# A 8192 x 8192 float32 transpose: eight column ranges of 16 KB regions and a looped TensorE program become four ranges of 32 KB regions, two load buffers, SyncE transfers and a written-out TensorE program

## The chip, the core and the metric

The kernel runs on one core of one Trainium2 chip. TensorE (PE), VectorE (DVE), ScalarE (ACT), GpSimd (POOL) and SyncE (SP) each run their own instruction stream and meet through semaphores; 16 DMA engines move data between HBM and SBUF, and every transfer here is cut into packets that are spread over all 16. The metric is the device time of one execution in microseconds, less is better.

## What is computed

The reference transposes a matrix and does nothing else:

```python
x = np.random.randn(8192, 8192).astype(np.float32)
def reference(x): return np.transpose(x)
```

256 MB are read and 256 MB are written.

## The kernel before

**Chunks.** The input is cut into 128 chunks of 128 rows by 4096 columns (2 MB each): the left half of the columns from top to bottom (64 chunks), then the right half. `chunks` (line 98) lists them. A load (lines 100 to 104) brings one chunk to SBUF, one row of 16 KB to each of the 128 partitions. There are three load buffers (`NIN`, line 65); the first three loads are issued by SP, all later ones by ACT, each after TensorE has finished the chunk that last used the buffer (lines 241 to 243), so load t+3 waits for chunk t.

**Transposes.** TensorE transposes a chunk in 32 blocks of 128 x 128 against an identity (line 118). Block b of a range takes every fourth column (`B` = 4), so that one partition of the result holds four output rows that lie side by side in HBM. The results of 16 transposes fill one half of PSUM (four banks); there are two halves, e = 0 and e = 1. TensorE's program is a loop, `turns` (lines 138 to 149), whose body holds the transposes of three chunks and is run 43 times; the waits are on semaphores that it counts down itself.

**Copies and regions.** ACT copies half 0 out of PSUM and DVE half 1 (line 228) to `regs`, nine regions of 16 KB per partition (`NREG`, line 66). The 4096 columns of a chunk are eight ranges q of 512 columns, and each range has one region open at a time. A region collects eight chunks (`W`), so that each output row piece is 8 x 128 x 4 B = 4 KB long. The ranges are staggered: range q closes when c mod 8 equals q (line 195), so one region closes, and one 2 MB store is issued, in every chunk. The ninth region is the one being stored; a range that reopens waits for the store that used the region last (lines 201 and 202). A window that runs over the end of the left half is stored in two parts. The first windows and the last ones are shorter.

**Stores.** `store` (line 160) issues on ACT, between its copies. `wide_dma` (line 20) hands the source to the transfer as one contiguous run per partition, and the destination as rows, so a 2 MB store reads 16 KB per partition and writes four rows of 4 KB. The very first store is an ordinary one.

So ACT's order of work in a chunk is: wait for PSUM and for a region, copy half 0, issue a store, wait for TensorE, issue a load. All loads from the fourth on, and all stores, go through ACT's one transfer queue and are taken in order. SBUF per partition: 3 x 16 KB of load buffers and 9 x 16 KB of regions, 192 KB.

Of the kernel before, what the change touches and what calls it, by code (L numbers as in the profile page):

```python
# [24 lines left out]
def wide_dma(nc, eng, queue, out, in_):  # L25


    return eng.add_instruction(
        mybir.InstDMACopy(
            mode="Copy",  # L30
            name=nc.get_next_instruction_name(),
            engine=eng.engine,
            ins=[physical(in_)],
            outs=[physical(out)],
            queue=queue,
        )
    )
# [3 lines left out]
def kernel(  # L41
# [5 lines left out]

    nc = tc.nc
    P = 128
    N, M = x.shape
    assert x.shape == out.shape[::-1]
    dt = x.dtype

    S = 32
    B = 4
    W = 8
    NR = S // B
    NIN = 3
    NREG = 9
    CH = N // P
    J = S * P

    with tc.tile_critical():  # L70
        nc.alloc_sbuf_tensor("pad", [P, 32], dt)
        ident = nc.alloc_sbuf_tensor("ident", [P, P], dt).ap()
        ins = [nc.alloc_sbuf_tensor(f"in{k}", [P, J], dt).ap() for k in range(NIN)]
        SIZE = B * W * P
        regs = nc.alloc_sbuf_tensor("regs", [P, NREG * SIZE], dt).ap()
        NH = NR // 2
        pss = [nc.alloc_psum_tensor(f"ps{k}", [P, NH * B * P], dt).ap() for k in range(2)]

        s_id = nc.alloc_semaphore("s_id")
        s_ld = [nc.alloc_semaphore(f"s_ld{k}") for k in range(NIN)]  # L80
        s_st = [nc.alloc_semaphore(f"s_st{k}") for k in range(NREG)]
        s_bank = [nc.alloc_semaphore("s_banka"), nc.alloc_semaphore("s_bankv")]
        s_pe = nc.alloc_semaphore("s_pe")
        s_cp = [nc.alloc_semaphore("s_cpa"), nc.alloc_semaphore("s_cpv")]

        nc.gpsimd.memset(ident, 0.0).then_inc(s_id, 1)  # L86
        nc.gpsimd.wait_ge(s_id, 1)
# [1 line left out]
            out=ident,  # L89
            in_=ident,  # L90
            compare_op=mybir.AluOpType.not_equal,
            fill=1.0,
            base=0,
# [1 line left out]
            channel_multiplier=1,  # L95
        ).then_inc(s_id, 1)

        chunks = [(s, c) for s in range(M // J) for c in range(CH)]

        def load(t):  # L100
            s, c = chunks[t]
            (nc.sync if t < NIN else nc.scalar).dma_start(
                out=ins[t % NIN], in_=x[c * P:(c + 1) * P, s * J:(s + 1) * J]
            ).then_inc(s_ld[t % NIN], 16)

        def transposes(k):
            nc.tensor.sem_inc(s_ld[k], -16).wait_op(s_ld[k], 16, "sem-ge")
            for q in range(NR):
                e, g = divmod(q, NH)
                if g == 0:
                    nc.tensor.sem_inc(s_bank[e], -1).wait_op(s_bank[e], 1, "sem-ge")  # L116
                for b in range(B):
                    tr = nc.tensor.transpose(  # L118
                        pss[e][:, (g * B + b) * P:(g * B + b + 1) * P],
                        ins[k][:, q * B * P + b:(q + 1) * B * P - B + b + 1:B],  # L120
                        ident,
                    )
                if q % 2:
                    tr.then_inc(s_pe, 1)

        T = len(chunks)
        assert T % NIN == NIN - 1
        pe = [nc.tensor.engine]  # L130
        for e in range(2):
            nc.tensor.sem_inc(s_bank[e], 1)
        nc.tensor.wait_ge(s_id, 2)

        turn = nc.alloc_registers("turn", engines=pe)
        nc.regs_mov(turn, 0)
        nc.br("turns", engines=pe)
        with nc.body("turns", valid_engines=pe):
            now = nc.snap(turn, min_val=0, max_val=T // NIN)
            with nc.tensor.If(now < 3):  # L140
                hint = nc.tensor.mark_branch_hint_location()
            with nc.tensor.If(now > 0):
                transposes(NIN - 1)
            for k in range(NIN - 1):
                transposes(k)
            nc.regs_alu(turn, turn, 1, op=mybir.AluOpType.add)
            nc.tensor.br_lt(
                turn, T // NIN + 1, on_true="turns", on_false="done"
            ).branch_hint(hint)
        nc.switch_bb("done")  # L150

        for t in range(NIN):
            load(t)

        copied = [0, 0]
        free = list(range(NREG))
        stored = [0] * NREG
        window = {}

        def store(q, e, count):  # L160
            t0, r, parts = window.pop(q)
            nc.scalar.wait_ge(s_cp[e], count)
            base = 0
            for s, a, z in parts:
                rows = (z - a) * P
                j0 = s * J + q * B * P
                dst = out[j0:j0 + B * P, a * P:a * P + rows]
                dst = dst.rearrange("(q b) i -> q b i", q=P)
                src = regs[:, r * SIZE + base:r * SIZE + base + B * rows]
                base += B * rows  # L170
                if any(stored):
                    st = wide_dma(nc, nc.scalar, "qActDynamicHW", dst, src)
                else:
                    st = nc.scalar.dma_start(
                        out=dst, in_=src.rearrange("q (b i) -> q b i", b=B)
                    )
                st.then_inc(s_st[r], 16)
                stored[r] += 1
            free.append(r)

        def closes(w, t):
            t0, r, parts = w
            return t + 1 == t0 + sum(z - a for _, a, z in parts)

        for t, (s, c) in enumerate(chunks):
            for e in range(2):
                eng = (nc.scalar, nc.vector)[e]

                place = []
                for q in range(e * NH, (e + 1) * NH):  # L190
                    if q not in window:

                        span = (q - c) % W + 1
                        r = free.pop(0)
                        parts = [(s, c, min(c + span, CH))]
                        if c + span > CH and t + span < T:
                            parts.append((s + 1, 0, c + span - CH))
                        window[q] = (t, r, parts)  # L200
                        if stored[r]:
                            eng.wait_ge(s_st[r], 16 * stored[r])
                    t0, r, parts = window[q]
                    k = [p[0] for p in parts].index(s)
                    base = r * SIZE + B * P * sum(z - a for _, a, z in parts[:k])
                    _, a, z = parts[k]
                    place.append((base + (c - a) * P, (z - a) * P))

                runs = []
                for g in range(NH):  # L210
                    if runs:
                        u = runs[-1]
                        gap = place[g][0] - place[g - 1][0]
                        if place[g][1] == place[u[0]][1] and abs(gap) < 2 ** 15 and (
                            len(u) == 1 or gap == place[u[1]][0] - place[u[0]][0]
                        ):
                            u.append(g)
                            continue
                    runs.append([g])
                for u in runs:  # L220
                    off, dist = place[u[0]]
                    gap = place[u[-1]][0] - place[u[-2]][0] if len(u) > 1 else 0
                    dims = [list(regs.ap[0]), [gap, len(u)], [dist, B], [1, P]]
                    o = bass.AP(regs.tensor, regs.offset + off, dims)
                    i = pss[e][:, u[0] * B * P:(u[-1] + 1) * B * P]
                    i = i.rearrange("p (l b i) -> p l b i", b=B, i=P)
                    eng.wait_ge(s_pe, t * NH + (e * NH + u[-1]) // 2 + 1)  # L227
                    cp = nc.scalar.copy(out=o, in_=i) if e == 0 else nc.vector.tensor_copy(out=o, in_=i)  # L228
                    ends = [e * NH + g for g in u if closes(window[e * NH + g], t)]
                    if ends:  # L230
                        cp.then_inc(s_cp[e], 1)
                        copied[e] += 1
                    if u is runs[-1]:
                        if ends:
                            eng.wait_ge(s_cp[e], copied[e])
                            eng.sem_inc(s_bank[e], 1)
                        else:
                            cp.then_inc(s_bank[e], 1)
                    for q in ends:
                        store(q, e, copied[e])  # L240
            if t + NIN < T:
                nc.scalar.wait_ge(s_pe, (t + 1) * NR // 2)
                load(t + NIN)
        for r in range(NREG):
            nc.sync.wait_ge(s_st[r], 16 * stored[r])

# [29 lines left out]
```

## Time and profile before

| what | value |
|---|---|
| median of three runs | 1263.73 us (1262.97 to 1264.22) |
| the profiled execution, first to last instruction (span) | 1261.2 us |
| TensorE busy with matmuls, 4096 of them | 740.3 us (59%) |
| VectorE busy, 250 copies | 302.7 us (24%) |
| ScalarE busy, 257 instructions | 252.6 us (20%) |
| loads, issued by SP and ACT | 128 of 2048 KB |
| stores, issued by ACT | 114 of 2048 KB, 28 smaller |
| HBM read, written | 268.44 MB each |
| mean granted TensorE clock | 0.751 |

The profiled execution has no runtime of its own beside its span; the runs' median lies 2.5 us above the span, which is taken as what a run has around its first and last instruction. Busy times are of single engines and overlap. "DMA" rows give the mean busy share of the 16 DMA engines and what they moved; a share a little over 1 means that the records of consecutive packets overlap by a few ns. A queue row has packets, MB, and the time of its packets as a share of 16 engines' time. Queue q10 is ACT's, q1 SP's; "instruction" queues carry program code to the engines' instruction memories, and not data.

### The profile page before, as it was taken

How to read it: one execution, taken by the hardware profiler on the slowest of the kernel's cores; microseconds unless marked ns; L12 is line 12 of the kernel's file. 1: busy time of each engine (PE TensorE's matmuls, PEld its weight loads, DVE VectorE, ACT ScalarE, POOL GpSimd, SP SyncE). 2: the span in 40 equal slices, each digit the busy share in tenths (PEclk: the TensorE clock that was granted, in tenths of full speed). 3: DMA queues.
4: the chain of work that ended last, by engine and by line, in shares of the span. 5: the costliest groups of instructions: out<-in, count | busy, mean ns of one | idle time of the engine just before them, and what ended most of it. 6: DMA issues, size and time to landing. Idle time of an engine off the chain costs nothing. (4 is left out here: it accounts for less than half of the span.)

```text
span 1261.2 us, 9840 instructions
## 1 busy us (share of the span) xinstructions
PE 740.3 (59%) x4096; PEld 719.8 (57%) x4096; DVE 302.7 (24%) x250; ACT 252.6 (20%) x257; POOL 0.7 (0%) x6
## 2 busy tenths in 40 slices
PE   6555655665556565665555655656566655656561
PEld 6555555665556555655555655656566655656561
DVE  3322222222222222222222222222222222222220
ACT  3212121121111211122211121121111211122120
POOL 0000000000000000000000000000000000000000
PEclk9987867777776868687776777676867677777866
DMA  9999999999999999999999999999999999999998
GB/s 386 429 427 426 430 427 429 431 428 430 431 428 431 429 429 430 430 429 430 425 423 419 431 430 429 430 430 429 431 430 429 431 429 430 430 430 429 429 429 351
DMA packets 39273, 536.97 MB, mean 426 GB/s; under 512 B 4320, under 2 KB 4832, under 8 KB 6240
## 3 DMA queue, kind: packets, MB, share of 16 engines
q10 hardware_dynamic: 38832, 530.60, 98.9%
q1 hardware_dynamic: 432, 6.29, 1.2%
q14 instruction: 8, 0.07, 0.0%
q8 instruction: 1, 0.02, 0.0%
HBM read 268.44 MB, written 268.44 MB: 426 GB/s over the span
## 5 line engine op out<-in xcount | busy, mean ns | idle before, releaser
L118 PE MATMUL ps<-ident,in 128*128 128x128 f32 x4096 | 740.3, 363 | 492.9 <-PEq L116 492.9
L118 PEld LDWEIGHTS ps<-ident,in 128*128 128x128 f32 x4096 | 719.8, 220 | 513.2 <-issue 513.2
L228 DVE COPY regs<-ps 128x512 f32<-128x512 f32 (+3 forms) x250 | 302.7, 1246 | 932.4 <-PE ps L118 780.2
L228 ACT COPY regs<-ps 128x512 f32<-128x512 f32 (+3 forms) x256 | 251.3, 1015 | 980.9 <-PE ps L118 495.5
L228 ACT ACT_TABLE_LOAD x1 | 1.3, 1283 | 0.9 <-SPq L70 0.9
L88 POOL TENSOR_SCALAR_AFFINE_SELECT ident<-ident 128x128 f32<-128x128 f32 x1 | 0.3, 292 | 0.2 <-POOL ident L86 0.2
L86 POOL MEMSET ident<- 128x128 f32 x1 | 0.2, 204 | 0.5 <-SPq L70 0.5
L260 POOL MEMSET const-bfloat16-1.0<- 128x1 bf16 x1 | 0.1, 101 | 0.0
L260 POOL MEMSET const-uint8-127<- 128x1 uint8 x1 | 0.1, 101 | 0.0
L260 POOL MEMSET const-float32-0.0<- 128x1 f32 x1 | 0.1, 98 | 0.2 <-issue 0.2
L260 POOL MEMSET const-float32-1.0<- 128x1 f32 x1 | 0.1, 98 | 0.0
## 6 DMA issues: line engine op xcount, KB each, us to landing
in<-in_x_dram ACTq DMA_DIRECT2D x125, 2048.0 KB, 21.7
out_dram<-regs ACTq DMA_DIRECT2D x114, 2048.0 KB, 17.5
out_dram<-regs ACTq DMA_DIRECT2D x4, 1792.0 KB, 17.1
in<-in_x_dram SPq DMA_DIRECT2D x3, 2048.0 KB, 11.6
out_dram<-regs ACTq DMA_DIRECT2D x4, 1536.0 KB, 15.2
out_dram<-regs ACTq DMA_DIRECT2D x4, 1280.0 KB, 15.5
out_dram<-regs ACTq DMA_DIRECT2D x4, 1024.0 KB, 15.6
out_dram<-regs ACTq DMA_DIRECT2D x4, 768.0 KB, 16.5
```

The lines of the kernel that those rows point to most:

```text
L86: nc.gpsimd.memset(ident, 0.0).then_inc(s_id, 1)
L88: nc.gpsimd.affine_select(out=ident, in_=ident, compare_op=mybir.AluOpType.not_equal, fill=1.0, base=0, pattern=[[-1, P]], channel_multipl ...
L118: tr = nc.tensor.transpose(pss[e][:, (g * B + b) * P:(g * B + b + 1) * P], ins[k][:, q * B * P + b:(q + 1) * B * P - B + b + 1:B], ident,)
L228: cp = nc.scalar.copy(out=o, in_=i) if e == 0 else nc.vector.tensor_copy(out=o, in_=i)
L260: nc = _bacc.Bacc("TRN2", target_bir_lowering=False, num_devices=1)
```

## The change

The sizes become `B` = 8, four ranges of 1024 columns (`NR` = 4), two load buffers, five regions of 32 KB. A range now closes in every second chunk (`STEP` = 2): range q closes when c mod 8 equals 2q+1. A full store is 4 MB, 32 KB read per partition and eight rows of 4 KB written. SBUF per partition stays 2 x 16 + 5 x 32 = 192 KB.

The third load that is issued at the start goes to the fifth region, which no range uses before chunk 2; load t+2 is issued when TensorE has finished chunk t, from t = 1 on. All loads and stores are issued by SP, in one order: for each chunk its load, then, when both the load is issued and the copies are done, the stores that close. ACT and DVE only copy. A copy is one instruction for two ranges where their places allow, else two.

TensorE's loop, its branch hint and the semaphores that it counted down are gone. The 4096 transposes are written out, each chunk with a wait for its load and, for each half of PSUM, a wait for the copy of the chunk before.

```diff
-    S = 32
-    B = 4
-    W = 8
+    S, B, W = 32, 8, 8
     NR = S // B
-    NIN = 3
-    NREG = 9
+    NH = NR // 2
+    STEP = W // NR
+    NREG = NR + 1
+    NIN = 2
...
-        with nc.body("turns", valid_engines=pe):
-            now = nc.snap(turn, min_val=0, max_val=T // NIN)
-            with nc.tensor.If(now < 3):
-                hint = nc.tensor.mark_branch_hint_location()
-            with nc.tensor.If(now > 0):
-                transposes(NIN - 1)
-            for k in range(NIN - 1):
-                transposes(k)
...
+        spare = regs[:, NR * SIZE:NR * SIZE + J]
+        slot = [(spare, s_ld[NIN], 16)]
+        for t in range(1, T):
+            k = t % NIN
+            slot.append((ins[k], s_ld[k], 16 * ((t + 1) // NIN if k else t // NIN)))
 
         def load(t):
             s, c = chunks[t]
-            (nc.sync if t < NIN else nc.scalar).dma_start(
-                out=ins[t % NIN], in_=x[c * P:(c + 1) * P, s * J:(s + 1) * J]
-            ).then_inc(s_ld[t % NIN], 16)
+            dst, sem, _ = slot[t]
+            nc.sync.dma_start(
+                out=dst, in_=x[c * P:(c + 1) * P, s * J:(s + 1) * J]
+            ).then_inc(sem, 16)
...
                 if any(stored):
-                    st = wide_dma(nc, nc.scalar, "qActDynamicHW", dst, src)
+                    st = wide_dma(nc, nc.sync, "qSPDynamicHW", dst, src)
...
+        def copy(t, e):
...
+                    span = (STEP * (q + 1) - 1 - c) % W + 1
...
+                    if stored[r]:
+                        eng.wait_ge(s_st[r], 16 * stored[r])
+                    elif r == NREG - 1:
+                        eng.wait_ge(s_pe, 2)
...
+            eng.wait_ge(s_pe, 2 * t + e + 1)
+            gap = place[1][0] - place[0][0]
+            whole = place[0][1] == place[1][1] and abs(gap) < 2 ** 15
+            for u in [range(NH)] if whole else [range(g, g + 1) for g in range(NH)]:
...
+            cp.then_inc(s_cp[e], 1)
+
+        for t in range(NIN + 1):
+            load(t)
+        nc.tensor.wait_ge(s_id, 2)
+        for t in range(T):
+            src, sem, count = slot[t]
+            nc.tensor.wait_ge(sem, count)
             for e in range(2):
+                if t:
+                    nc.tensor.wait_ge(s_cp[e], t)
                 for g in range(NH):
+                    for b in range(B):
+                        o = (g * B + b) * P
+                        i = (e * NH + g) * B * P + b
+                        tr = nc.tensor.transpose(
+                            pss[e][:, o:o + P], src[:, i:i + B * (P - 1) + 1:B], ident
+                        )
+                tr.then_inc(s_pe, 1)
+                copy(t, e)
+            if t and t + NIN < T:
+                nc.sync.wait_ge(s_pe, 2 * (t + 1))
                 load(t + NIN)
+            done = [
+                q for q, (t0, _, parts) in window.items()
+                if t + 1 == t0 + sum(z - a for _, a, z in parts)
+            ]
+            for e in sorted({q // NH for q in done}):
+                nc.sync.wait_ge(s_cp[e], t + 1)
+            for q in sorted(done):
+                store(q)
```

## The prediction

> **What bounds the kernel now.** I read the page's first three parts, then stretches of the span, then the transfers, then the order of time.
>
> ```profile
> span 1261.2 us, 9840 instructions
> PE 740.3 (59%) x4096; PEld 719.8 (57%) x4096; DVE 302.7 (24%) x250; ACT 252.6 (20%) x257; POOL 0.7 (0%) x6
> DMA  9999999999999999999999999999999999999998
> DMA packets 39273, 536.97 MB, mean 426 GB/s; under 512 B 4320, under 2 KB 4832, under 8 KB 6240
> q10 hardware_dynamic: 38832, 530.60, 98.9%
> q14 instruction: 8, 0.07, 0.0%
> q8 instruction: 1, 0.02, 0.0%
> ```
>
> No compute engine is busy for more than 59%, while the 16 DMA engines are full from the first slice to the last but one. The kernel is bound by its transfers, and the change moves the same bytes. Stretches of the span say how evenly (us, then each engine's busy time, clock, DMA share, GB/s):
>
> ```profile
> 0.00:15.00 15.00, 6.54 (x41) 6.57 (x42) 1.78 (x3) 3.43 (x5) 0.70 (x6) 1.00 0.89 364
> 600.00:690.00 90.00, 51.76 (x288) 50.31 (x288) 22.16 (x33) 17.92 (x21) 0.00 (x0) 0.75 1.01 422
> 690.00:1200.00 510.00, 308.57 (x1671) 300.20 (x1672) 121.66 (x81) 101.30 (x95) 0.00 (x0) 0.74 1.01 430
> 1230.00:1255.20 25.20, 3.22 (x24) 3.03 (x22) 2.48 (x4) 2.29 (x4) 0.00 (x0) 0.64 0.99 414
> 1255.20:1261.20 6.00, 0.00 (x0) 0.00 (x0) 0.00 (x0) 0.00 (x0) 0.00 (x0) 0.50 0.18 76
> ```
>
> The steady rate is 430 GB/s; the middle, where windows are split between the halves of the matrix, is at 422. In the last 6 us only some engines still work (share 0.18). The timeline gives the period:
>
> ```profile
> 1198.67 6.13 PE L118 MATMUL ps<-ident,in 128*128 128x128 f32 x32 [4.19 <-PEq L116]
> 1208.44 6.34 PE L118 MATMUL ps<-ident,in 128*128 128x128 f32 x32 [3.63 <-PEq L116]
> 1218.22 6.54 PE L118 MATMUL ps<-ident,in 128*128 128x128 f32 x32 [3.44 <-PEq L116]
> ```
>
> A chunk comes every 9.77 us, half of it load (4.87) and half store (4.9); TensorE uses 4.1 to 6.5 of it. What ends last is thus the DMA engine with the most work. The landing records of a transfer have 16 entries, one per DMA engine: they lie within 0.4 us of each other at 80 us, but 5.3 us apart at 700 us and until the end (the last transfer: median 1255.6, last 1259.9). One engine is late, and the end waits for it: **work that falls on one DMA engine counts in full, work spread over 16 counts a sixteenth.**
>
> **The code fetch.** So the two instruction queues need a closer look, though their share rounds to 0.0%. Narrow stretches of the DMA view (84.7 to 85.8 us, then 378.2 to 378.6 us):
>
> ```profile
> q8 instruction: 1, 0.02, 5.7%
> q14 instruction: 1, 0.01, 4.8%
> ```
>
> 5.7% of 16 engines in 1.1 us is 1.00 us for one block of 16 KB, in one packet on one DMA engine; 4.8% in 0.4 us is 0.31 us for a block of 8 KB. After the first, the spread of the landings goes from 0.4 to 1.8 us within one transfer. After an 8 KB block the next data packet takes 796 or about 1035 ns instead of 611, so such a block costs its engine 0.31 + 0.19 = 0.50 or 0.31 + 0.42 = 0.73 us. The eight small blocks come at 97, 200, 378, 619, 626, 878, 1149 and 1168 us. ACT's program has 633 recorded instructions and DVE's 357, which at 128 per block gives one in 255 and one in 452 us: 97, 378, 626, 878, 1168 fit ACT, 200, 619, 1149 fit DVE, and 8192 B per 128 instructions is 64 B each. Following the packets of each DMA engine end to end, 378 and 626 are on the same engine, 878 and 1168 are on the same engine, and 200 and 619 are on the same other one. So each program's code comes through one DMA engine. TensorE's 8805 executed instructions are nearly absent here: its loop body of three chunks stays in its memory.
>
> **The change, part by part** (against the span of 1261.2 us).
>
> *TensorE written out.* 4096 transposes are 8192 instructions (4096 weight loads, 4096 matmuls), with 128 waits for loads and 254 for copies 8575; at 64 B 549 KB, 33.5 blocks of 16 KB. By the 16 KB row 33.5 x 1.00 = 33.5 us on one DMA engine. The engine that is now last is 4.3 us behind the median, and I assume TensorE's to be another: net +29.2. Upper bound: 67 blocks of 8 KB at 0.73 = 49, and the same engine as today's last, so +49. Lower bound: spread over all 16, 33.5 / 16 = +2.1, or 0 if the block fell into idle time, of which the DMA rows show none. I take 29.2, since the only 16 KB block has its own row and blocks of one program stay on one engine. The fetch does not stall TensorE itself: 256 instructions last four chunks (39 us), and TensorE waits over 3 us in each.
>
> The Trainium skill, "Runtime: NRT & Kernel Launch", section "Instruction fetch mechanics", says that the next page of code is fetched while the current one runs, that crossing a block is "mostly hidden", and that full unrolling is preferable to taken branches. By that the term would be near 0; it looks at the engine that runs the code, and the landings here show the cost on the DMA engine that carries it.
>
> *Larger stores.* A packet of 16 KB takes 611 ns (loads and some stores) or 616 (other stores), one of 4 KB 159 or 165; the line through them leaves 8 to 15 ns per packet, of which 3 to 4 overlap with the next. One 32 KB packet for two saves 5 to 11 ns if this is per packet, nothing if it is per 4 KB row. 1024 store packets per engine become 512: 0 to -5.6 us. Packets of 2 KB in four rows of 512 B take 84 to 89, with the same rest, which speaks for per packet: I take -3, with it 72 fewer transfers' completion packets of 9 ns.
>
> *Splits in the middle.* 90 x (1 - 422/430) = 1.7 us are lost there for seven split windows; three remain, -1.0 (0 to -1.7).
>
> *The start.* Load 3 was issued at 14.18 us, after chunk 0. It now waits for chunk 1, whose transposes ended at 18.03 us, while the data of the first three loads ends at 17.5 us. First bytes came 1.0 us after issue (0.94 to 1.9): 19.1 - 17.5 = +1.6 (0 to +3, the latter if chunk 1 takes 5.57 us, as chunk 3 did, for 4.1). The 1 MB store behind load 3 covers the wait for load 4.
>
> *The steady part.* Load t+2 waits for chunk t, queued behind nothing but the SP wait. Let the DMA engines start load t+1 (t odd) at X: load t+2 runs from X+4.9, the 4 MB store of chunk t from X+9.7 to X+19.5. Chunk t had landed before the previous store began, so it ends by X-1, and load t+2 is in the queue 4.9 us early. Chunk t+1 lands at X+5.5 and ends by X+12; load t+3 is 6 us early. A reopened region's store ended at X, and its copy starts after X+5.5. Cover 4.9 us, cost 0; without it every us late counts once in two chunks, 62 times. ACT's 0.55 us per store and 0.3 to 0.6 per load move to SP, which is free: 0. Chunk copies wait for 16 transposes and not for single ranges, hidden by the same cover.
>
> *The end.* The last 4 MB store covers the last two chunks (2 x 5.6 us), their copies (2.3) and the issue (1.0): first bytes at X+20.0 against X+19.5, +0.5 (0 to +2).
>
> Sum: 29.2 - 3 - 1.0 + 1.6 + 0.5 = +27.3, a span of 1288.5; with the 2.5 us that the runs' median lies above the span, **1291 us**, 2.2% slower.
>
> **Rivals.** *Spread code:* TensorE's blocks rotate over the DMA engines. For it: only one block of its queue was seen. Against: ACT's and DVE's stay put. 2.1 - 3 - 1.0 + 1.6 + 0.5 = +0.2, 1264 us.
>
> *Larger packets win:* the fixed part of a packet is fully per packet (-5.6, splits -1.7) and code costs under 1.7 us, because it is hidden or spread; with start and end at 2.1 the sum is down to -5.2, 1259 us. It decides once code costs less than the 2.7 us that separate it from no change at -2.5. This is also what the Trainium skill's page on the runtime would lead to. Against: a row of 1.00 us per block, and shares of 1.01 that leave no idle time.
>
> *Late loads:* with two buffers the cover of 4.9 us is used up, because SP's issue blocks: ACT's load at 627.18 us took 4.59 us to issue behind two store parts, and a 4 MB store has twice the rows. If 0.5 us stayed uncovered in each of 62 pairs, +31 on top: 1322 us. Against: the block there let go while a store part was still running, so the queue never ran dry.
>
> **Chances and range.** Forecast 0.72, its own range 1278 (eight blocks held in memory from the start, -8, and the low ends) to 1318 (code at 49, the high ends). Spread code 0.12, larger packets 0.09, late loads 0.07. The 8-in-10 range reaches down to spread code and leaves out the larger packets, the late loads and the forecast's top: 1263 to 1308. A measurement of this kernel tells about 0.2% (2.5 us) from no change. Faster 0.10 (larger packets, a little of spread code), same 0.11, slower 0.79.
>
> **What would show it.** About 33 blocks of 16 KB (or 67 of 8 KB), some 0.55 MB, on an instruction queue; landings of a transfer spread until one DMA engine is steadily last; the mean DMA share a few per cent below 1.01 and about 420 GB/s in the steady part, a chunk every 10.0 us. Store packets near 1215 to 1225 ns for 32 KB. A gap of 1 to 3 us near 18 us. It is wrong if code packets are on many engines, if the steady rate stays at 430 or more, or if SP waits at issues while DMA engines idle together.

## The result and the profile after

The changed kernel takes 1271.15 us (median of four runs, 1270.15 to 1272.03) against 1263.97 us of the kernel before on the same chip (four runs): ratio 1.0057, 95% interval 1.0045 to 1.0069. So it is 7.2 us slower. The profiled execution has a span of 1270.2 us, 9.0 us more than the 1261.2 of before. Each run lies 1.8 us above its own span; the profiled execution of the kernel before was the fastest of its runs (1262.97 us) and that of the changed kernel the slowest (1272.03), so the spans lie somewhat further apart than the medians. The forecast was 27 us.

The page of the changed kernel, first and third part (busy times, the DMA row in 40 slices, queues):

```profile
span 1270.2 us, 8969 instructions
PE 624.5 (49%) x4096; PEld 595.2 (47%) x4096; DVE 295.2 (23%) x156; ACT 242.6 (19%) x167; POOL 0.7 (0%) x6
DMA  8999999999999999999999999999999999999998
GB/s 330 382 424 426 432 427 430 431 428 434 429 424 435 424 430 433 424 433 428 429 425 427 430 429 426 433 425 431 432 425 432 425 420 433 426 431 433 424 431 354
DMA packets 29446, 537.46 MB, mean 423 GB/s; under 512 B 3168, under 2 KB 4192, under 8 KB 4192
q1 hardware_dynamic: 29408, 536.88, 99.5%
q8 instruction: 32, 0.52, 0.2%
q14 instruction: 6, 0.05, 0.0%
```

The DMA engines are still the bound: no compute engine is over 49%. Queue q8 now carries 32 blocks of TensorE's code, 0.52 MB, where before it had one. And the loss sits at the left edge: the first slice is an 8, and the first two slices move 330 and 382 GB/s. The GB/s row of the kernel before starts with 386 and 429:

```profile
GB/s 386 429 427 426 430 427 429 431 428 430 431 428 431 429 429 430 430 429 430 425 423 419 431 430 429 430 430 429 431 430 429 431 429 430 430 430 429 429 429 351
```

Stretches of the changed kernel (us, busy time of PE, PEld, DVE, ACT, POOL, granted clock, DMA share, GB/s):

```profile
0.00:15.00 15.00, 6.61 (x39) 6.64 (x40) 0.54 (x1) 3.21 (x3) 0.70 (x6) 1.00 0.87 357
15.00:30.00 15.00, 7.69 (x62) 7.11 (x62) 6.53 (x6) 3.86 (x4) 0.00 (x0) 0.89 0.83 288
30.00:60.00 30.00, 19.93 (x127) 19.16 (x125) 7.75 (x7) 7.71 (x8) 0.00 (x0) 0.83 0.95 380
600.00:690.00 90.00, 47.71 (x308) 45.68 (x309) 21.14 (x17) 18.29 (x16) 0.00 (x0) 0.75 1.01 428
690.00:1200.00 510.00, 256.03 (x1678) 243.89 (x1676) 119.56 (x58) 98.34 (x61) 0.00 (x0) 0.76 1.01 428
1264.20:1270.20 6.00, 0.00 (x0) 0.00 (x0) 0.00 (x0) 0.00 (x0) 0.00 (x0) 0.50 0.44 188
```

The same early stretches of the kernel before:

```profile
15.00:30.00 15.00, 12.70 (x89) 12.19 (x88) 6.87 (x12) 6.38 (x11) 0.00 (x0) 0.89 0.99 399
30.00:60.00 30.00, 17.83 (x129) 17.18 (x128) 10.43 (x16) 8.00 (x8) 0.00 (x0) 0.94 1.02 431
```

From 15 to 60 us the changed kernel moves 288 and 380 GB/s where 399 and 431 were moved: (399 - 288) x 15 + (431 - 380) x 30 = 3.2 MB, which take 7.5 us at 429 GB/s. In the long stretch after 690 us the rates are 428 and 430, and in the middle 428 and 422. The timeline of the changed kernel says what happens at the start (start, length, engine, line, operation, and in brackets the idle time before it and what ended it):

```profile
16.87 3.83 PE L183 MATMUL ps<-ident,in 128*128 128x128 f32 x32 [0.65 <-DVE regs L166]
18.94 0.33 SPq L105 DMA_DIRECT2D in<-in_x_dram  x1
...
23.44 12.12 SPq L105 DMA_DIRECT2D in<-in_x_dram  x2
...
29.43 5.78 PE L183 MATMUL ps<-ident,in 128*128 128x128 f32 x32 [6.01 <-DMA in<-in_x_dram]
...
35.61 0.58 SPq L28 DMA_DIRECT2D out_dram<-regs  x1
36.81 3.86 PE L183 MATMUL ps<-ident,in 128*128 128x128 f32 x32 [1.61 <-DMA in<-in_x_dram]
```

The data of the three first loads ends at 17.6 us. Load 3 is issued at 18.94, after chunk 1, and its first packets start at 19.9; from 17.6 to 19.9 no data moves. Of its 128 packets of 16 KB, 63 then take the usual 0.61 us and 39 take 1.0 to 1.5 us; the mean is 0.84, so that an engine's eight packets take 6.7 us instead of 4.9. TensorE waits 6.0 us for the load, and load 5, which waits for that chunk, is late in turn. (It is the second of the two issues in the row that starts at 23.44, and starts at 35.24.) From 34.6 to 36.0 us most engines are idle, and over a third of load 5's packets take 1 us or more again. One pause costs three times: the gap, the slow packets after it, and the next load.

**An account of the span.** To set the terms side by side, the durations of all packets were added up and divided by the 16 engines: data packets at up to 1.05 times the median of their size; what longer packets took beyond that ("slow"); code blocks; the rest is idle time (3.5 ns per packet are taken off, by which consecutive packets overlap). In us of the span:

| kernel | span | data packets | slow, first 60 us | slow, later | code | idle, first 60 us | idle, middle | idle, last 35 us |
|---|---|---|---|---|---|---|---|---|
| before | 1261.2 | 1251.0 | 1.1 | 1.8 | 0.2 | 2.4 | -0.2 | 4.9 |
| after | 1270.2 | 1250.8 | 4.0 | 2.1 | 2.2 | 7.0 | -0.3 | 4.4 |
| before, loop written out | 1265.6 | 1251.1 | 1.5 | 2.2 | 2.2 | 2.4 | 0.7 | 5.6 |
| after, two loads at start | 1270.0 | 1250.8 | 4.5 | 1.6 | 2.1 | 6.0 | -0.3 | 5.4 |
| after, four loads | 1264.6 | 1250.7 | 2.8 | 1.9 | 2.1 | 2.9 | -0.2 | 4.4 |
| after, five loads | 1264.8 | 1250.7 | 3.1 | 1.7 | 2.1 | 2.7 | -0.3 | 4.9 |
| after, six loads | 1266.8 | 1250.8 | 3.0 | 2.1 | 2.2 | 4.3 | -0.2 | 4.7 |
| after, stores in halves | 1272.9 | 1251.7 | 4.4 | 4.0 | 2.1 | 5.1 | 0.0 | 5.7 |
| after, loop of two chunks | 1277.7 | 1251.4 | 3.9 | 8.5 | 0.2 | 6.1 | 0.4 | 7.3 |
| six loads, loop | 1270.6 | 1250.7 | 3.3 | 4.8 | 0.2 | 4.9 | -0.2 | 6.9 |
| six loads, loop, half the transposes | 1260.5 | 1250.2 | 3.3 | 0.9 | 0.2 | 2.6 | -0.3 | 3.6 |
| five loads, loop, 48 more transposes | 1270.0 | 1250.9 | 4.3 | 3.5 | 0.3 | 3.8 | -0.2 | 7.4 |

Of the 9.0 us between before and after, the start is 7.5 (idle +4.6, slow packets +2.9), code 2.0, all else -0.5. It is one execution each; the medians of runs lie 7.2 us apart.

### The profile page after: what moved, and what is told of

Its sections match the earlier page's. It is cut to its first block, busy times and chain, and to the rows that moved or that the text cites. A ratio compares the mean times of both kernels' runs of the same rounds, so it can differ in the third digit from the quotient of the medians.

```text
span 1270.2 us, 8969 instructions
## 1 busy us (share of the span) xinstructions
PE 624.5 (49%) x4096; PEld 595.2 (47%) x4096; DVE 295.2 (23%) x156; ACT 242.6 (19%) x167; POOL 0.7 (0%) x6
## 4 chain that ended last, share of the span: by engine, by line
DMA 67%; PE 29%; DVE 1%; issue 0%; SPq 0%; DVEq 0%
DMA in<-in_x_dram 67%; PE ps L183 29%; DVE regs L166 1%; DMA regs<-in_x_dram 1%; SPq L226 0%; DVEq L154 0%; SPq L67 0%
## 5 line engine op out<-in xcount | busy, mean ns | idle before, releaser
L183 PE MATMUL ps<-ident,in 128*128 128x128 f32 x4064 | 618.6, 322 | 605.8 <-DMA in<-in_x_dram 573.3
L183 PEld LDWEIGHTS ps<-ident,in 128*128 128x128 f32 x4064 | 589.4, 202 | 634.8 <-DMA in<-in_x_dram 585.9
L166 DVE COPY regs<-ps 128x2048 f32<-128x2048 f32 (+1 forms) x156 | 295.2, 1907 | 945.8 <-PE ps L183 945.8
L164 ACT COPY regs<-ps 128x2048 f32<-128x2048 f32 (+1 forms) x166 | 241.3, 1477 | 994.9 <-PE ps L183 994.9
L183 PE MATMUL ps<-ident,regs 128*128 128x128 f32 x32 | 6.0, 377 | 8.4 <-DMA regs<-in_x_dram 8.4
L183 PEld LDWEIGHTS ps<-ident,regs 128*128 128x128 f32 x32 | 5.9, 218 | 8.4 <-issue 8.4
```

Of the source, the lines that this page charges most:

```text
L166: cp = nc.vector.tensor_copy(out=o, in_=i)
L183: tr = nc.tensor.transpose(pss[e][:, o:o + P], src[:, i:i + B * (P - 1) + 1:B], ident)
```

## The experiments

Unless another kernel is named, each edit is made to the changed kernel (1271.15 us). The kernel before took 1263.8 to 1264.4 us beside them. A ratio is to that kernel, run on the same chip as the experiment; the experiments ran on several chips, so small differences between two of them are read from the ratios.

**TensorE's loop written out, alone, in the kernel before.** The 43 passes over `transposes` are issued one after the other, and nothing else changes:

```diff
-        with nc.body("turns", valid_engines=pe):
...
+        for t in range(T):
+            transposes(t % NIN)
```

> The kernel before with TensorE's loop written out, that part of the change alone. Theory of the start: 8 DMA engines get four blocks of about 1 us each, which adds 1 to 4 us to the slowest, 1265 to 1268. What the prediction said (one DMA engine): 29 us more, 1293. If written-out code were the whole of the change's loss: 7 us more, 1271.

Measured 1267.42 us (11 runs, 1267.11 to 1268.69) against 1264.38: ratio 1.0024 (1.0015 to 1.0033), +3.0 us; not 1293. The page's third part has the blocks:

```profile
q10 hardware_dynamic: 38832, 530.60, 98.6%
q1 hardware_dynamic: 432, 6.29, 1.2%
q8 instruction: 33, 0.54, 0.2%
```

33 blocks, 0.54 MB: the amount that was forecast, at a tenth of the price. Why is seen in the landings of one load near 900 us (us after the first of the 16 DMA engines, sorted; worked out from the completion records):

```
before, at 940        latest four  3.2, 3.4, 3.8, 5.3
before, written out   0 .2 .3 .6 .9 1.1 2.2 3.0 | 4.7 4.9 5.0 5.3 5.4 5.6 6.2 6.2
after                 0 .1 .1 .2 .2 .3 .5 | 2.6 2.7 3.7 3.7 3.9 4.4 4.7 4.9 5.1
after, loop of two    0 .1 .2 .2 .3 .3 .4 1.0 1.2 1.3 1.4 1.4 1.6 3.2 3.3 6.4
```

With the code written out, half of the engines fall behind together: eight are 4.7 to 6.2 us late in the kernel before, nine are 2.6 to 5.1 us late in the changed one. With the loop, one engine is late by itself. The blocks' own durations tell the same: in the changed kernel they read, in order of time from 789 us, 951, 951, 1007, 1002, 994, 1032, 1032, 1020, 951, 951, 1007, 1007 ns: a pattern that returns with every eighth block. The landings show it too. Their distances stay nearly the same from transfer to transfer, except that each block puts one engine back. In the kernel before, written out, six blocks from 726 to 911 us put back six different engines, and the blocks eight later, from 1021 to 1216 us, the same six in the same order; in the changed kernel the blocks at 789, 828, 866 and 905 us are followed on the same engines by those at 1102, 1141, 1180 and 1219. The DMA view of the changed kernel from 135.5 to 136.6 us has one such block:

```profile
q1 hardware_dynamic: 19, 0.54, 117.2%
q8 instruction: 1, 0.02, 5.8%
```

The same view from 439.3 to 440.4 us has the block that came eight blocks later:

```profile
q1 hardware_dynamic: 30, 0.46, 100.0%
q8 instruction: 1, 0.02, 5.8%
```

5.8% of 16 engines in 1.1 us is 1.02 us for the block itself, as forecast. But the data packet behind a block is slow as well. In the kernel before, written out, the packets behind the ten blocks from 726 to 1059 us take 0.98 to 1.16 us where 0.61 is usual; in the changed kernel those of 32 KB behind the blocks from 789 to 1063 us take 1.59 to 1.64 where 1.23 is. Together a block puts its engine 1.3 to 1.7 us back in the landings, about 1.5. The account has the second part under slow packets, and not under code. Four blocks fall on each of eight engines, some 6 us. The mean over all 16 engines is 33 x 1.5 / 16 = 3.1 us, an estimate from these rows, and the run measured 3.0: the cost is near the mean, and far from the sum on one engine. How much of the lateness of single engines reaches the end was not followed further.

**TensorE's loop put back into the changed kernel**, two chunks per pass, with the semaphores that count down:

```diff
...
+        with nc.body("turns", valid_engines=pe):
...
+            for k in range(2):
+                transposes(ins[k], s_ld[k])
...
```

> The changed kernel with TensorE's transposes in a loop of two chunks (the first two chunks written out), as the kernel before had it; all else stays. Theory of the start: the 32 blocks of code fall on 8 DMA engines in turn, four blocks of 1.0 us on each, so that the loop saves 2 to 4 us, 1267 to 1269. Rival, the written-out code as the whole cause: 7 us or more are saved, 1264 or less. What the prediction said, all code on one DMA engine: some 29 us. Theory of the steady part: nothing is saved, 1271.

Measured 1274.76 us (5 runs, 1273.08 to 1279.48), ratio 1.0077 (1.0063 to 1.009): 3.6 us slower than written out by the medians, not 2 to 4 us faster (the intervals of the two ratios just touch; the runs' ranges don't). The expectation failed. The profiled run is the longest of the five, so the account overstates it, but it shows the place: code falls by 2.0 us, slow packets after the start rise by 6.4, idle time at the end by 2.9. The long stretch of this run is at 424 GB/s. One engine alone is 6.4 us behind (last row of the landings above).

**Four loads at the start.** Chunks 0 and 1 go to the two halves of the fifth region, chunks 2 and 3 to the load buffers:

```diff
-        spare = regs[:, NR * SIZE:NR * SIZE + J]
-        slot = [(spare, s_ld[NIN], 16)]
+        spare = [regs[:, NR * SIZE + k * J:NR * SIZE + (k + 1) * J] for k in range(2)]
+        slot = [(spare[k], s_ld[NIN + k], 16) for k in range(2)]
...
-            if t and t + NIN < T:
+            if t > 1 and t + NIN < T:
```

> Four loads are issued at the start instead of three: chunks 0 and 1 go to the two halves of the fifth region, chunks 2 and 3 to the two load buffers. Theory of the start: of the 9.0 us by which the profiled span grew, some 7.7 lie in the first 60 us (about 357, 288 and 380 GB/s there against 364, 399 and 431 before), because load 3 waits for chunk 1 and loads 5 and 7 then wait for the chunks behind it. With four loads in the queue the gap at 17.4 us closes, and the time falls by 6 to 8 us, from 1271 to about 1264. Rival, the written-out code: its 0.5 MB is the cause, the start is a symptom that is made up later, and the time stays at 1271 within 2 us. Rival, the steady part: one queue of SyncE and two buffers lose a little in each pair of chunks; then too the time stays at 1269 or more.

Measured 1267.32 us (11 runs, 1265.42 to 1268.43), ratio 1.002 (1.0011 to 1.0029): 3.8 us better by medians, 5.6 by the spans. The gain stayed below the 6 to 8 us that were expected. In the account the start gives back 5.3 us (idle 7.0 to 2.9, slow packets 4.0 to 2.8), the rest is unchanged. So more than half of the change's loss is the start, and it is a matter of which loads are ahead.

**Stores in two halves.** Each 4 MB store is issued as two transfers of 16 KB per partition, so that the packets have the old size:

```diff
-                    st = wide_dma(nc, nc.sync, "qSPDynamicHW", dst, src)
+                    for h in range(2):
+                        st = wide_dma(
+                            nc, nc.sync, "qSPDynamicHW", dst[:, h * 4:h * 4 + 4],
+                            src[:, h * 4 * rows:(h + 1) * 4 * rows],
+                        )
...
```

> The changed kernel with every store but the first cut into two transfers of four rows per partition, so that packets are 16 KB again and regions, waits and order stay. A 32 KB packet in the changed kernel takes 1228 ns, twice 614: if the fixed part is per 4 KB row, the halves cost 0 to 2 us more, 1271 to 1273. What the prediction took (5 to 11 ns saved per packet pair): 3 to 5.6 us more, 1274 to 1277.

Measured 1274.85 us (5 runs, 1274.66 to 1275.63), ratio 1.0081 (1.0067 to 1.0095), 3.7 us slower by the medians (the intervals of the two ratios just touch), inside the second range. But the account doesn't bear out the reason: the data packets themselves are only 0.9 us more, and 2.3 us are slow packets, 1.3 idle time at the end. And from before to after, where packets went from 16 to 32 KB as well, the data packets changed by 0.2 us. Between 200 and 600 us a 16 KB packet of before takes 613.2 ns in the mean; in the changed kernel a 16 KB one takes 611.7 and a 32 KB one 1227.2, which is 613.6 for 16 KB. Over a load and a store that is 1 ns less for 32 KB, and one overlap of 3.5 ns with the packet before is gone with it, so the larger packet saves nothing. What halving the stores costs is mostly slow packets. The cover defined further down is shorter in this run (by 0.3 us on average, with ten pairs under 3 us where the changed kernel has five), which fits, but why it is shorter is left open.

**Two loads at the start**, without the one in the fifth region:

```diff
-        slot = [(spare, s_ld[NIN], 16)]
-        for t in range(1, T):
+        slot = []
+        for t in range(T):
...
```

> The changed kernel (1271.2 us) without its first load in the fifth region: two loads ahead of chunk 0, load 2 waits for chunk 0 and load 3 for chunk 1. Theory (each late load at the start leaves all DMA engines idle for its wait and the packets after it slow): the data of two loads ends at 12.6 us, chunk 0 ends near 14 us and its load's first bytes come 1.8 us later, so a gap of some 3 us moves from 17.4 to 12.6 us, a further one follows, and the load that was ahead is missing: 2 to 5 us slower than the changed kernel, 1273 to 1276 us. Rival (the prediction's working, a gap is only the time to the first byte): 15.2 - 12.6 = 2.6 us in place of 1.6, so 1272 us.

Measured 1273.31 us (6 runs, 1271.35 to 1274.76), ratio 1.0066 (1.0046 to 1.0085); the interval overlaps that of the changed kernel, and the profiled span, 1270.0, is no longer. Inconclusive between the two, and the upper end of what was expected is excluded. Against the kernel before it is 8.9 us slower, the changed kernel 7.2: the load ahead in the unused region is worth some 1.7 us, not clear of noise.

**Six and five loads at the start.** Chunks 2 and 3 (in the second run only chunk 2) go to the upper halves of regions 0 and 1, which the first short windows leave empty:

```diff
+        spare = [regs[:, o:o + J] for o in (NR * SIZE, NR * SIZE + J, J, SIZE + J)]
...
-            if t and t + NIN < T:
+            if t > 3 and t + NIN < T:
```

> The changed kernel with six loads at the start: chunks 0 and 1 in the two halves of the fifth region, chunks 2 and 3 in the upper halves of regions 0 and 1, which the first short windows leave empty, chunks 4 and 5 in the two load buffers. Theory (what is left of the start's loss with four loads, 402 GB/s at 30 to 60 us, is loads that wait for buffers): stretches 15 to 30 and 30 to 60 us at 400 to 430 GB/s, 2 to 4 us less than the 1267.3 of four loads, 1263.5 to 1265.5 us. Rival (the rest comes from the short first windows with their 1 and 2 MB stores, or from the first chunks' transposes): no more than 1 us better, 1266.3 us or more.

> The written-out changed kernel with five loads at the start: chunks 0 and 1 in the fifth region, chunk 2 in the upper half of region 0, chunks 3 and 4 in the two load buffers. With six loads the copies of chunk 4 waited for region 0, whose 1 MB store stood behind all six loads (landed at 36 us and later, TensorE idle until 40.7 us). With five loads that store should land near 31 us and load 5 be issued before the store ends. If so, 400 GB/s or more in both stretches 15 to 30 and 30 to 60 us, and 1264 to 1266 us (four loads 1267.3, six 1269.0). Rival (chunk by chunk TensorE and the copies are no faster than the loads at the start, so something waits at any depth): within 1 us of four loads, 1266.3 us or more.

Six loads: 1269.03 us (12 runs), ratio 1.0033 (1.0022 to 1.0043), a miss. The first gap is gone (433 GB/s from 15 to 30 us), but a new one opens (362 GB/s from 30 to 60 us). The timeline of this run:

```profile
29.23 3.83 PE L183 MATMUL ps<-ident,in 128*128 128x128 f32 x32 [1.02 <-DMA in<-in_x_dram]
...
38.59 1.93 ACT L164 COPY regs<-ps 128x1024 f32<-128x1024 f32 x2 [11.11 <-DMA out_dram<-regs]
40.66 5.57 PE L183 MATMUL ps<-ident,in 128*128 128x128 f32 x32 [7.60 <-ACT regs L164]
```

ACT waits 11.1 us for a store: region 0 has to be written out before chunk 4 can be copied into it, and its store stands in the one queue behind all six loads. TensorE then waits 7.6 us for the copy, and load 7 for TensorE. With five loads that wait is gone, and the time is 1266.57 us (11 runs, 1265.33 to 1267.40), ratio 1.0017 (1.0008 to 1.0026): 0.75 us under four loads, which can't be told from none, so the rival of that expectation was nearer. The rates came to 391 and 402 GB/s, not to 400 in both stretches. What else holds the start back was not found.

**Why the loop was slower.** The six-load kernel was run with the loop, and with a loop that makes only half of each chunk's transposes:

```diff
...
-                transposes(ins[k], s_ld[k])
+                transposes(ins[k], s_ld[k], B // 2)
```

> Six loads at the start, and TensorE's program as a loop of two chunks after the first four, as in the run with the loop before. Theory late loads (without code blocks that rotate over the DMA engines one engine falls 6 us behind, its chunk starts late, and the next load is issued too late for the engines that are ahead): the stretch from 700 to 1200 us at 422 to 427 GB/s, not faster than the written-out kernel with six loads, 1265 to 1268 us. Rival (code costs 3 us and nothing takes its place; the slow run with the loop had another cause at the start): 429 GB/s or more there, 1260 to 1262 us.

> The same loop with half of the transposes of each chunk left out after the first four chunks (the other half of the output holds old values); all transfers and copies are as before. Theory late loads: TensorE ends a chunk some 3 us sooner, each load is issued that much earlier, and the stretch from 700 to 1200 us returns to 429 to 431 GB/s, 2 us or more faster than the loop with all transposes. Rival (the slow packets of the loop's run have nothing to do with the time of the loads): the same rate within 1 GB/s and the same time within 1 us as the loop with all transposes.

The loop: 1272.36 us (6 runs, 1271.39 to 1273.62), ratio 1.0058 (1.004 to 1.0077), 3.3 us slower than the same kernel written out, beyond the range but in the direction of late loads. With half of the transposes: 1262.36 us (12 runs, 1261.37 to 1263.38), 10.0 us faster and 430 GB/s, as its theory had it; half of its output is not computed. The transfers and copies are the same. What differs is the moment at which loads are issued, and that TensorE reads and writes half as much. The stretch from 700 to 1200 us of the loop:

```profile
700.00:1200.00 500.00, 252.76 (x1658) 242.05 (x1656) 117.66 (x58) 97.59 (x60) 0.00 (x0) 0.76 1.00 427
```

and of the loop with half the transposes:

```profile
700.00:1200.00 500.00, 162.00 (x808) 145.76 (x806) 117.27 (x57) 95.30 (x59) 0.00 (x0) 0.64 1.00 430
```

The rate is 430 GB/s in place of 427, which is 3.5 us over the 500; by the account most of the rest of the 10 us lies at the start (2.3) and at the end (3.3). The timeline of the loop (SPq L106 is the load that follows the chunk):

```profile
875.03 7.76 PE L142 MATMUL ps<-ident,in 128*128 128x128 f32 x48 [9.73 <-PEq L137]
...
880.80 4.81 SPq L106 DMA_DIRECT2D in<-in_x_dram  x2
```

and of the loop with half:

```profile
868.34 3.53 PE L142 MATMUL ps<-ident,in 128*128 128x128 f32 x16 [11.01 <-PEq L137]
...
871.90 3.94 SPq L106 DMA_DIRECT2D in<-in_x_dram  x2
```

From the start of the chunk to the issue of the load it is 5.8 us in the one and 3.6 in the other. For each pair of chunks in nine of the kernels I took the cover, from the issue of the pair's first load until the foremost engine ends the store ahead of it, and the time that slow packets (16 KB over 640 ns, 32 KB over 1300) cost in the following 20 us:

| cover, us | pairs | slow packets per pair, us (mean of 16 engines) |
|---|---|---|
| under 2.5 | 13 | 0.37 |
| 2.5 to 3 | 43 | 0.22 |
| 3 to 3.5 | 48 | 0.03 |
| 3.5 to 5 | 180 | 0.01 |
| over 5 | 174 | 0.02 |

Under 3 us of cover, packets become slow. Cover shrinks by what the latest engine is behind, because a chunk starts when the last of 16 engines has landed: 4.5 us of lag and 4.4 of cover in the changed kernel on average, 4.8 and 4.0 in its loop form, 3.0 and 7.8 with half the transposes. That packets are slow where the cover is short is shown by the table. That the lag of one engine is what makes the loop slower is an inference, and the six-load pair speaks against it in part: written out and looped, the mean lag is 4.5 us in both, and after 690 us it is 5.1 and 5.3. That earlier loads, and not less traffic of TensorE, remove the loss is not separated by the half loop alone; the next run, with more work for TensorE, bears on it.

**TensorE kept at work.** After its pause of 9 us TensorE makes the first transposes of a pair in 213 ns each and, some 4 us later, when the granted clock goes to 1.0, in 110. So 48 transposes of the identity were put ahead of each pair (with five loads at the start, in the loop):

```diff
+            for e in range(2):
+                nc.tensor.wait_ge(s_bank[e], 1)
+            for b in range(48):
+                nc.tensor.transpose(pss[0][:, b % B * P:(b % B + 1) * P], ident, ident)
             for k in range(2):
                 transposes(ins[k], s_ld[k])
```

> Five loads at the start, TensorE's loop of two chunks, and 48 transposes of the identity ahead of each pair of chunks, whose result is overwritten: TensorE is then at work until shortly before the pair's first chunk lands. Theory (late loads; the first 4 us of transposes after a long pause run at 213 ns each in place of 110, so the first chunk of a pair takes 6.2 us in place of 3.7, and the load behind it comes too late for the DMA engines that are ahead): with TensorE kept at work the chunk ends 2 us or more sooner, the stretch from 700 to 1200 us comes to 429 GB/s or more (427 without), and the time is 1261 to 1264 us, below the kernel before (1264.4). Rival (the extra work changes nothing in the transfers, or delays the first chunk): 427 GB/s or less, 1268 us or more.

Measured 1271.59 us (5 runs, 1270.63 to 1271.80), ratio 1.0057 (1.0043 to 1.0071): a miss. Its timeline:

```profile
906.34 5.43 PE L163 MATMUL ps<-ident 128*128 128x128 f32 x48 [2.53 <-DVEq L216]
913.59 3.77 PE L142 MATMUL ps<-ident,in 128*128 128x128 f32 x32 [1.82 <-PEq L137]
...
917.39 5.20 SPq L106 DMA_DIRECT2D in<-in_x_dram  x2
```

A pair's first chunk does come down to 3.8 us in 41 of 62 pairs, with a pause of up to 1.82 us before it (once 2.13); in the other 21 it takes 5.2 to 5.4 us, after pauses of 1.86 to 3.15 us. Mean cover rose to 5.3 us and slow packets after the start were 3.5 us, where the six-load loop without this work had 4.8: fewer, with more traffic of TensorE and earlier loads, which speaks for the moment of the load. But one engine got still further behind (6.8 us at 898 us), and the last 35 us hold 7.4 us of idle time against 4.9 in the written-out kernel with five loads. Against that kernel the start also costs 2.3 us more and slow packets later 1.8 more, while code costs 1.8 less. So the late engine is a part of what was lost, and not all of it.

**SyncE alone, in the kernel before:** all transfers and the waits ahead of them move from ACT to SP.

```diff
-                    st = wide_dma(nc, nc.scalar, "qActDynamicHW", dst, src)
+                    st = wide_dma(nc, nc.sync, "qSPDynamicHW", dst, src)
...
-                nc.scalar.wait_ge(s_pe, (t + 1) * NR // 2)
+                nc.sync.wait_ge(s_pe, (t + 1) * NR // 2)
```

> The kernel before with one part of the change alone: all loads and stores, and the waits ahead of them, are issued by SyncE in place of ScalarE. Theory (the prediction's step: the issue costs move to an engine that is free, cost 0; the DMA engines are the bound): 1263.5 to 1265.5 us, no difference to 1264.3. Rival (ScalarE's copies come sooner once it no longer waits at issues, or SyncE's waits in one row hold a load back behind a store): more than 1.5 us to either side, a gain of 1.5 to 3 us if the copies' delay had cost transfers, a loss of 2 us or more if SyncE blocks.

Measured 1264.61 us (11 runs) against 1263.75: ratio 1.001 (0.9997 to 1.0023). No difference that can be told (-0.4 to 2.9 us by the interval), as expected.

No version with the right output beat the kernel before; the best, five loads at the start and the code written out, is 2.3 us behind it.

## Why the prediction was right and wrong

**Code, +29.2: the step that failed.** "Each program's code comes through one DMA engine" was read from the five blocks of ACT and the three of DVE, of which four and two could be placed on an engine. TensorE's blocks go over eight engines in turn. Number (32 for 33.5) and size (16 KB) of the blocks held. The multiplier was wrong, 1 in place of 1/16. The price of 1.0 us was the block's packet alone; with the slow packet behind it a block costs its engine about 1.5 us, and the landings that the prediction quotes had it (0.4 to 1.8 us, a step of 1.4). It measured 2.0 us in the account, without those packets, and 3.0 in the run with that part alone. The rival "spread code" had put it at 2.1. The rows of other engines' programs were no evidence for this one, and its only block of before could not show a rotation; the bounds of the estimate, 2.1 and 49, said so, and the value chosen between them did not.

The Trainium skill, "Runtime: NRT & Kernel Launch", section "Instruction fetch mechanics", calls the crossing of a block mostly hidden. That is nearer to these runs than my step was, but it isn't free: 3.0 us (1.9 to 4.2 by the interval) for 0.5 MB in a kernel that its transfers bound.

**The start, +1.6 (0 to +3): the second step that failed.** It measured 7.5 in the account, and five loads gave 4.6 us of medians back. The step priced one gap to the first byte, and that part was right: 17.6 to 19.9 us is 2.3, inside its range. It left out that load 3's packets are slow after the pause (0.84 us in the mean for 0.61), and that chunk 3, and with it load 5, waits for load 3: "the 1 MB store behind load 3 covers the wait for load 4" was true, but the next wait was load 5's.

**Larger stores, -3 (0 to -5.6): mis-sized.** All data packets together are -0.2. The line through two packet sizes gave 8 to 15 ns per packet that a packet of twice the size does not save: 1227.2 ns is twice 613.6, where one of 16 KB took 613.2 before.

**Splits in the middle, -1.0: held.** 428 for 422 GB/s in 90 us is 1.3 us. In the account most of it is slow packets that are gone (0.9 us between 600 and 690 us before, 0.05 after).

**The steady part, 0: nearly held, with less to spare than thought.** The cover of 4.9 us was measured at 4.4 on average, and at 3.5 after 690 us. Slow packets after 690 us are 1.3 us where the kernel before had 0.04 and, with its code written out, 0.5; so short cover costs somewhat under 1 us here. The rival "late loads" named the right place, cover that is used up, but by another cause: SyncE's issues did not block (under 0.7 us each between 60 and 1240 us, but for one of 1.9), and no cost of issuing by SyncE could be told in the run with that part alone. What the runs show instead is that packets grow slow at less than 3 us of cover.

**The end, +0.5: small, as said, but of the other sign.** Idle time in the last 35 us is 4.4 us against 4.9, so -0.5, outside the range of 0 to +2.

Put together: the forecast's terms 29.2, -3, -1.0, +1.6, +0.5 became in the account +2.0 for code, -0.2 for data packets, +7.5 at the start, -0.5 at the end, +0.3 for slow packets later (splits, blocks and late loads together) and -0.1 between, which is the span's 9.0. The runs that take parts away agree: the code alone costs 3.0 us, and five loads at the start leave 2.3 of the 7.2. Only the loop put back does not fit the sum: it should have won 2 to 3 us and lost 3.6, and why stays open. The forecast's sign was luck. With the code's cost as it is, its own terms come to +1.1 us (3.0 in place of 29.2), less than the 2.5 us that it could tell from no change; the slowdown came out of the start, a small term of the sum, and not out of the term that made it.

## What to carry to other kernels

Program code is a transfer too: count its blocks, but find out over how many DMA engines they go before multiplying, since the factor can be 16, and read a block's price from how far it puts its engine back, and not from its own packet. When load buffers are taken away, walk the first six chunks by hand until the stores have filled the queue, and follow each late load to the next one that waits for it; free space in regions not yet in use can hold first loads, as long as no store that others wait for stands behind them. In these kernels, which are bound by their transfers, a load had to be issued some 3 us before the foremost engine needed it, and the lag of the latest of the 16 engines eats into that.

## What the runs showed of the hardware

- Blocks of TensorE's program rotate over eight of the 16 DMA engines, 0.94 to 1.04 us each after the first, with the same durations every eighth block. The data packet behind a block is slow too (0.98 to 1.16 us for 0.61), so that a block puts its engine some 1.5 us back.
- After a pause of all DMA engines (17.6 to 19.9 us), 39 of the next load's 128 packets of 16 KB took 1.0 to 1.5 us in place of 0.61, at its start and again near its end. Why was not tried.
- The engine that is last in the loop kernels takes 1242 to 1259 ns in the mean for its 32 KB store packets between 480 and 1200 us, the foremost 1224 to 1226, so it falls further behind, by 3 us between 486 and 894 us in the run with the additional transposes. Why was not tried either.
- A transpose of 128 x 128 took 213 ns after a pause of 9 us and 110 ns after some 4 us of work. The Trainium skill, "TensorE: Matmul & The Clock Gate", section "Why this matters for your kernels", asks for no pause over about 3 us between bursts. Here that was not enough: pauses up to 1.82 us kept the fast rate, but of the 22 pauses from 1.86 to 3.15 us 21 lost it, and keeping the rate in the other pairs did not make this kernel faster.
